# Hymba trunk on one core: quad blocks that accumulate in a kept PSUM bank

## The chip, the core and the metric

The kernel runs on one core of a Trainium2 chip. A time is the device time of one execution in microseconds (us). The kernel before takes 909.75 us, the median of three runs (909.21 to 910.25). Of the engines, TensorE (PE) multiplies, VectorE (DVE) does elementwise arithmetic, ScalarE (ACT) copies and applies functions, GpSimd (POOL) and SyncE (SP) mostly start transfers. Products of TensorE land in PSUM, which the program uses as eight banks of 128 x 512 float32.

## What is computed

Two layers work on 256 tokens of width 1024. Each layer is a half-step feed-forward network (FFN), a mixer of three kinds of heads, and a second half-step FFN, each between two norms:

```python
def _swiglu(h, wg, wu, wd):
    return (jax.nn.silu(h @ wg) * (h @ wu)) @ wd

for l in range(DEPTH):        # DEPTH = 2, D_MODEL = 1024, D_FF = 2816, 256 tokens
    f = _swiglu(_rmsnorm(h, ff1_norm_pre[l]), ff1_w_gate[l], ff1_w_up[l], ff1_w_down[l])
    h = h + 0.5 * _rmsnorm(f, ff1_norm_post[l])
    m = _hybrid_mixer(_rmsnorm(h, mix_norm_pre[l]), ...)
    h = h + _rmsnorm(m, mix_norm_post[l])
    f = _swiglu(_rmsnorm(h, ff2_norm_pre[l]), ff2_w_gate[l], ff2_w_up[l], ff2_w_down[l])
    h = h + 0.5 * _rmsnorm(f, ff2_norm_post[l])
```

## The kernel before

There are four FFNs: FFN1 and FFN2 around the mixer of layer 0, FFN3 and FFN4 around that of layer 1. The gate and up projections have 2816 columns, worked on as 11 units of 256. Units 0 and 1 go first (`ffn_first`); then come three quad blocks of two units each, which begin at units 2, 5 and 8 (`ffn_quad`), and after each of them a pair, which is one unit: 4, 7 and 10 (`ffn_pair`, and `ffn_last_pair` for unit 10). The down projections of a block (`down`, `mm_rows`, L412) run in the block behind it and accumulate in four banks with the tag "acc". All else uses four banks with the tag "wk", handed out in turn.

A float32 product is made of three TensorE products of split operands: the high half (`hi`) of the weights is written by ScalarE (L114), the low half (`lo`) by VectorE (L115) as weights less `hi`; hi·hi, lo·hi and hi·lo accumulate in one bank. The weights' splits are called by `W.pump`, which loads and splits as far as slots are free; `raw`, `hi` and `lo` have five slots each. `pump_behind(m)` places such a call behind the instruction m.

A quad block multiplies a 2 x 2 block of activations by a 2 x 2 block of weights with seven products instead of eight. Each is one call of `product` (L592, its matmul is L598), with sums of activations on the left (`X11`, `S1` to `S4`, `X12`, `X22`) and sums of weights (`g1`, `T1` to `T4`, `g2`, `u2`) on the right; the sums of weights are made by VectorE (L113). Before, four banks are used, in this order of the text: pa takes X11·g1, and ScalarE copies it to `w2` (L609). pc takes S1·T1, copied to `h1` (L614). pb takes S2·T2, and VectorE adds it to `w2` (L625); the sum is subtracted from pc (L626). pd takes S3·T3, and VectorE adds `w2` to it (L637) and subtracts it from `h1` (L638). Then X12·g2 is accumulated onto pa, X22·T4 onto pd, S4·u2 onto pc; ScalarE applies Silu to pa (L647) and pd (L658), VectorE multiplies (L659, L669). The block of unit 8 is called late: its downs are placed otherwise.

The last pair multiplies with the weights on the moving side (`mm_side`). Unit 10's gate columns, then its up columns, each in two halves j = 0 and 1; a half is eight matmuls 512 wide (L359) and eight 256 wide (L361) into one bank. ScalarE copies one part of the bank out (L364), VectorE adds the other (L365). The last pair's activations then go to the downs of the FFN's end.

Results of a block are turned for the downs by a transfer: `send` has ScalarE part the halves of each number (L515) and starts a transposing DMA, `receive` puts them together (L528) and splits them (ScalarE L250, VectorE L251).

A scheduler sets the order on each engine: it starts from the text, estimates durations and may move an instruction of one engine ahead of another where no dependence and no `issue_after` or `keep_in_program_order` speaks against it. A pool gives out banks in turn, and a matmul that starts a bank anew waits until the last reader of what stood there is done.

Of the kernel before, what the change touches and what calls it, by code (L numbers as in the profile page):

```python
# [10 lines left out]
F32 = mybir.dt.float32  # L11
# [23 lines left out]
TAIL = 4  # L35

# [125 lines left out]
def hybrid_trunk_kernel(ctx: ExitStack, tc: tile.TileContext, a, out: bass.AP):  # L162
# [16 lines left out]
    def bank(tag="wk"):  # L179
        return psum.tile([P, 512], F32, tag=tag, name=f"{tag}{next(ids)}")  # L180
# [171 lines left out]
    def mm_side(u, out, between=None):  # L352

        hi, lo = (w[:, :UNIT].rearrange("p (k n) -> p k n", k=KD) for w in W.get(u))
        for j in range(2):
            s = slice(j * P, (j + 1) * P)
            ps = bank()
            for k in range(KD):
                nc.tensor.matmul(ps, hi[:, k, s], both[:, :, k, :], start=k == 0, stop=k == KD - 1)  # L359
            for k in range(KD):  # L360
                mm_side.end = nc.tensor.matmul(ps[:, S:], lo[:, k, s], xT[0][:, k, :], start=False, stop=k == KD - 1,  # L361
                                               skip_group_check=True)
            o = out[:, j * S : (j + 1) * S]
            nc.scalar.activation(o, ps[:, S:], AF.Copy)  # L364
            mm_side.last = nc.vector.tensor_tensor(o, ps[:, :S], o, op=ALU.add)  # L365
            if between and not j:
                between()
        W.done(u)
        return out
# [28 lines left out]
    def mm_rows(acc, u, t, xs, first, last, between=None, at=6, span=(0, 12), pin=False):  # L398

        hi, lo = (w[:, :UNIT].rearrange("p (j n) -> p j n", j=2) for w in W.get(u))  # L400
        if isinstance(xs, dict):
            s = slice(None)
            xh, xl = (x.rearrange("p (j n) -> p j n", n=P)[:, xs["at"] : xs["at"] + 2] for x in xs[t])
# [80 lines left out]
    def ffn_first(t, p, pin=False, ahead=None, between=None, by_dma=False):  # L484

        ps = [bank(), bank()]
# [24 lines left out]
    def send(x, more=False):  # L511

        n = 2 * x.shape[1]
        halves = buf(U16, n)
        part = send.last = nc.scalar.activation(halves.rearrange("p (a n) -> p a n", a=2),  # L515
                                    x[:, :].bitcast(U16).rearrange("p (n a) -> p a n", a=2), AF.Copy)
        turned = buf(U16, n)
        with tc.issue_after(part.ins):
            t = send.dma = nc.sync.dma_start_transpose(turned.rearrange("p (a n) -> p a n", n=P), halves)
        if W.allowed < 10 and not more:  # L520
            W.allowed, W.behind = 10**6, t.ins
        return turned

    def receive(turned):

        n = turned.shape[1] // 2
        x = buf(n=n)
        nc.scalar.activation(x[:, :].bitcast(U16).rearrange("p (n a) -> p a n", a=2), turned.rearrange("p (a n) -> p a n", a=2),  # L528
                             AF.Copy)
        hT = (buf(F32R, n), buf(F32R, n))  # L530
# [13 lines left out]
    def ffn_pair(i, p, turn, take):  # L544

        ps = [bank(), bank()]
# [55 lines left out]
    def ffn_quad(i, p, left, turn, downs, by_dma, two, take=None):  # L602
# [5 lines left out]
        w2 = buf()  # L608
        nc.scalar.activation(w2, pa, AF.Copy)  # L609
# [13 lines left out]
        pb = bank()  # L623
        product(pb, left["S2"], p["T2", i], True)
        nc.vector.tensor_tensor(w2, pb, w2, op=ALU.add)  # L625
# [7 lines left out]
        if not late:  # L633
            downs[0]()
        pd = bank()
        product(pd, left["S3"], p["T3", i], True)
        nc.vector.tensor_tensor(pd, pd, w2, op=ALU.add)  # L637
# [7 lines left out]
        product(pa, left["X12"], p["g2", i], False)  # L645
        h0 = buf()
        nc.scalar.activation(h0, pa, AF.Silu)  # L647
# [33 lines left out]
    def ffn(l, n, p, gain, turned, left, next_left, before_next, last, later=None):  # L681
# [22 lines left out]
        def both(i, behind=None, order=(0, 1)):  # L704
# [5 lines left out]
            else:  # L710
                down(i, 0, behind)
# [53 lines left out]
        xn0 = None if last else before_next(0)  # L765
        for i in range(NU - TAIL, NU):
            if i == NU - 1 and not last:
                pre_turn(0, xn0, left=next_left)
            down(i, 1)
# [7 lines left out]
        W.pump(SPLIT_BUFS - 1)  # L777
# [32 lines left out]
    def mixer(l, p, turned, next_left, before_next):  # L810
# [4 lines left out]
        def first(t, ahead=None):  # L815
            pq, pkv = bank(), bank()
# [62 lines left out]
        def taps(name, tile0):  # L879
            ps = bank()  # L880
# [87 lines left out]
        ps = bank()  # L968
# [58 lines left out]
        pu = bank()  # L1027
# [56 lines left out]
        def zed(t):  # L1084
            ps = bank()
# [39 lines left out]
        def scan(t):  # L1125
            ps = bank()
# [18 lines left out]
        def gated_turn(t, yn):  # L1145
            ps = bank()
# [223 lines left out]
```

## Time and profile before

| | before |
|---|---|
| median of three runs | 909.75 us |
| the profiled execution's own time | 908.51 us |
| its span, first to last instruction | 906.8 us |
| TensorE's mean granted clock | 0.999 of full speed |
| mean DMA rate | 221 GB/s |

A line of a group in the profile names the line of the code, the engine, the operation, the tiles by name (output <- input, numbers left out), shapes and count, then the busy time in us and the mean of one in ns, then the engine's idle time just ahead of it and what ended most of it. A line of a timeline gives start and duration in us of a stretch of instructions, and in brackets the idle time ahead of it. Matmuls are pipelined: a duration of 0.39 us is the way through, and in a row one starts every 0.227 us (256 columns: 0.12). VectorE's and ScalarE's durations overlap a little with the next one's as well.

### The profile page before, as it was taken

How to read it: one execution, taken by the hardware profiler on the slowest of the kernel's cores; microseconds unless marked ns; L12 is line 12 of the kernel's file. 1: busy time of each engine (PE TensorE's matmuls, PEld its weight loads, DVE VectorE, ACT ScalarE, POOL GpSimd, SP SyncE). 2: the span in 40 equal slices, each digit the busy share in tenths (PEclk: the TensorE clock that was granted, in tenths of full speed). 3: DMA queues.
4: the chain of work that ended last, by engine and by line, in shares of the span. 5: the costliest groups of instructions: out<-in, count | busy, mean ns of one | idle time of the engine just before them, and what ended most of it. 6: DMA issues, size and time to landing. Idle time of an engine off the chain costs nothing.

```text
span 906.8 us, 12010 instructions
## 1 busy us (share of the span) xinstructions
PE 897.8 (99%) x4428; PEld 753.8 (83%) x4428; DVE 792.6 (87%) x1044; ACT 673.9 (74%) x1037; POOL 29.9 (3%) x49
## 2 busy tenths in 40 slices
PE   8999999999999999999999999999999999999997
PEld 5888888889988888888888888888998888888885
DVE  6999978899878998988799989888989699989982
ACT  7776776878858777787868678767796668778762
POOL 0000000000001000000000000000000110000000
PEclk9999999999999999999999999999999999999999
DMA  9679888865345489779665978795825256978731
GB/s 365 190 275 265 355 194 278 258 235 183 104 174 219 115 317 228 280 194 284 228 197 152 329 211 299 191 304 212 295 99 166 90 174 182 337 212 299 201 115 47
DMA packets 69326, 200.70 MB, mean 221 GB/s; under 512 B 44306, under 2 KB 44818, under 8 KB 47252
## 3 DMA queue, kind: packets, MB, share of 16 engines
q1 hardware_dynamic: 67396, 187.23, 61.0%
q0 software_dynamic: 1728, 12.58, 7.5%
q8 instruction: 35, 0.57, 0.3%
q14 instruction: 23, 0.19, 0.1%
q10 hardware_dynamic: 144, 0.13, 0.0%
HBM read 188.65 MB, written 1.05 MB: 209 GB/s over the span
## 4 chain that ended last, share of the span: by engine, by line
PE 93%; DVE 4%; issue 2%; ACT 0%; POOLq 0%; POOL 0%; DVEq 0%
PE acc L412 29%; PE wk L598 24%; PE wk L390 13%; PE wk L555 10%; PE wk L350 6%; PE wk L359 3%; DVE lo L115 2%; PE wk L361 2%; PE wk L377 1%; PE wk L301 1%; PE wk L1130 1%; PE acc L873 0%; PE acc L225 0%; DVE raw L113 0%; PE acc L943 0%
## 5 line engine op out<-in xcount | busy, mean ns | idle before, releaser
L115 DVE TENSOR_TENSOR lo<-raw,hi 128x1024 fp32r<-128x1024 f32 (+2 forms) x452 | 465.0, 1079 | 35.1 <-ACT hi L114 34.3
L114 ACT ACTIVATE hi<-raw 128x1024 fp32r<-128x1024 f32 (+2 forms) x452 | 399.1, 937 | 62.4 <-DVE raw L113 26.3
L412 PE MATMUL acc<-hi,t 128*128 128x512 f32 x832 | 214.7, 390 | 0.0
L412 PEld LDWEIGHTS acc<-hi,t 128*128 128x128 f32 x832 | 155.1, 188 | 31.9 <-DVE t L251 0.2
L412 PE MATMUL acc<-lo,t 128*128 128x512 f32 x416 | 113.5, 390 | 0.0
L598 PE MATMUL wk<-hi,n 128*128 128x512 f32 x384 | 100.5, 390 | 0.0
L390 PE MATMUL wk<-hi,xT 128*128 128x512 f32 x384 | 98.6, 393 | 0.0
L412 PEld LDWEIGHTS acc<-lo,t 128*128 128x128 f32 x416 | 78.0, 188 | 16.3
L598 PEld LDWEIGHTS wk<-hi,n 128*128 128x128 f32 x384 | 71.8, 188 | 14.8
L390 PEld LDWEIGHTS wk<-hi,xT 128*128 128x128 f32 x384 | 71.0, 188 | 15.6 <-ACT xT L250 0.7
L598 PE MATMUL wk<-hi,xT 128*128 128x512 f32 x288 | 77.1, 389 | 0.1
L515 ACT ACTIVATE t<-t 128x1024 uint16<-128x1024 uint16 x39 | 41.2, 1056 | 43.7 <-DVE t L669 23.3
L113 DVE TENSOR_TENSOR raw<-raw,raw 128x1024 f32<-128x1024 f32 x56 | 67.0, 1220 | 0.1
L555 PE MATMUL wk<-hi,xT 128*128 128x512 f32 x256 | 64.5, 389 | 0.0
L598 PEld LDWEIGHTS wk<-hi,xT 128*128 128x128 f32 x288 | 54.0, 188 | 11.6 <-DVE t L638 0.4
L555 PEld LDWEIGHTS wk<-hi,xT 128*128 128x128 f32 x256 | 48.1, 188 | 10.0
L528 ACT ACTIVATE t<-t 128x1024 uint16<-128x1024 uint16 x35 | 47.8, 1367 | 8.7 <-DMA t<-t 8.6
L598 PE MATMUL wk<-lo,n 128*128 128x512 f32 x192 | 52.1, 390 | 0.0
L390 PE MATMUL wk<-lo,xT 128*128 128x512 f32 x192 | 52.0, 391 | 0.0
L390 PEld LDWEIGHTS wk<-lo,xT 128*128 128x128 f32 x192 | 36.0, 188 | 8.3 <-DVE lo L115 0.8
L350 PE MATMUL wk<-xT,hi 128*128 128x256 f32 x320 | 42.5, 284 | 0.0
L598 PEld LDWEIGHTS wk<-lo,n 128*128 128x128 f32 x192 | 36.0, 188 | 7.8 <-DVE lo L115 0.2
(190 smaller groups left out, 994.7 us busy)
## 6 DMA issues: line engine op xcount, KB each, us to landing
raw<-in_ff_q SPq DMA_DIRECT2D x48, 1024.0 KB, 6.6
raw<-in_ff_d SPq DMA_DIRECT2D x44, 1024.0 KB, 5.1
raw<-in_ff_f SPq DMA_DIRECT2D x16, 1024.0 KB, 7.2
raw<-in_ff_p SPq DMA_DIRECT2D x16, 1024.0 KB, 4.8
raw<-in_ff_q POOLq DMA_DIRECT2D x12, 1024.0 KB, 8.2
raw<-in_w_in SPq DMA_DIRECT2D x10, 1024.0 KB, 5.1
raw<-in_w_kvz SPq DMA_DIRECT2D x8, 1024.0 KB, 6.7
raw<-in_w_out SPq DMA_DIRECT2D x8, 1024.0 KB, 5.3
```

The lines of the kernel that those rows point to most:

```text
L113: nc.vector.tensor_tensor(raw[:, s], self.raw[x][:, s], self.raw[y][:, s], op=op)
L114: self.act = nc.scalar.activation(hi[:, s], raw[:, s], AF.Copy)
L115: nc.vector.tensor_tensor(lo[:, s], raw[:, s], hi[:, s].bitcast(F32), op=ALU.subtract)
L350: nc.tensor.matmul(ps, w[:, k, s], y[:, k, :], start=i == 0 and k == 0, stop=i == 2 and k == KD - 1)
L359: nc.tensor.matmul(ps, hi[:, k, s], both[:, :, k, :], start=k == 0, stop=k == KD - 1)
L361: mm_side.end = nc.tensor.matmul(ps[:, S:], lo[:, k, s], xT[0][:, k, :], start=False, stop=k == KD - 1, skip_group_check=True)
L390: m = nc.tensor.matmul(ps, y[:, k, :], w[:, k, :], start=h == 0 and n == 0, stop=h == 1 and n == len(parts) - 1)
L412: m = nc.tensor.matmul(acc[b], x[:, j, s], w[:, j, b * 512 : (b + 1) * 512], start=first and j == 0 and i == 0, stop=last and j == 1 and i ...
L515: part = send.last = nc.scalar.activation(halves.rearrange("p (a n) -> p a n", a=2), x[:, :].bitcast(U16).rearrange("p (n a) -> p a n", a= ...
L528: nc.scalar.activation(x[:, :].bitcast(U16).rearrange("p (n a) -> p a n", a=2), turned.rearrange("p (a n) -> p a n", a=2), AF.Copy)
L555: m = nc.tensor.matmul(ps[t], y[:, c, :], w[:, c, :], start=k == 0 and n == 0, stop=k == 1 and n == len(parts) - 1)
L598: nc.tensor.matmul(ps, x[:, k, :], w[:, k, :], start=first and n == 0, stop=n == len(parts) - 1, skip_group_check=not first)
```

## The change

It has five parts. First, the four banks of "wk" become three and one bank with a tag of its own, "keep". Second, in the quad blocks that aren't late (units 2 and 5), X11·g1 still goes to pa, but ScalarE copies it into the kept bank pe instead of `w2`. S2·T2 accumulates onto pa, ScalarE copies the sum from pa to a new `w2`, S3·T3 accumulates onto pa too, and X12·g2 accumulates onto the kept bank pe. VectorE's two additions aren't needed there. Third, the late block stays as it was, with the kept bank for pb. Fourth, the other users of "wk" take the kept bank for one of their banks: the first one in `ffn_first`, the second in `ffn_pair` and in the mixer's `first`, the second half of each unit in `mm_side`, and each fourth bank elsewhere in the mixer (`mbank`). Fifth, the downs of an FFN's last units for the second half of the tokens are placed behind those for the first half, and the call of `W.pump` at the end is placed behind the first half's norm. The code of `send` and `receive` loses a size that is always the same.

```diff
+BANKS = {"wk": 3, "keep": 1, "acc": 4}
...
     def bank(tag="wk"):
-        return psum.tile([P, 512], F32, tag=tag, name=f"{tag}{next(ids)}")
+        return psum.tile([P, 512], F32, tag=tag, name=f"{tag}{next(ids)}", bufs=BANKS[tag])
+
+    turns = iter(range(10**6))
+
+    def mbank():
+        return bank("keep" if next(turns) % 4 == 3 else "wk")
...
         for j in range(2):                                   # mm_side
             s = slice(j * P, (j + 1) * P)
-            ps = bank()
+            ps = bank("keep" if j else "wk")
...
-        ps = [bank(), bank()]                                # ffn_first
+        ps = [bank("keep"), bank()]
...
-        ps = [bank(), bank()]                                # ffn_pair
+        ps = [bank(), bank("keep")]
...
         product(pa, left["X11"], p["g1", i], True)           # ffn_quad
-        w2 = buf()
-        nc.scalar.activation(w2, pa, AF.Copy)
+        pe = w2 = buf() if late else bank("keep")
+        nc.scalar.activation(pe, pa, AF.Copy)
...
-        pb = bank()
-        product(pb, left["S2"], p["T2", i], True)
-        nc.vector.tensor_tensor(w2, pb, w2, op=ALU.add)
+        if late:
+            pb = bank("keep")
+            product(pb, left["S2"], p["T2", i], True)
+            nc.vector.tensor_tensor(w2, pb, w2, op=ALU.add)
+        else:
+            product(pa, left["S2"], p["T2", i], False)
+            w2 = buf()
+            nc.scalar.activation(w2, pa, AF.Copy)
         m = nc.vector.tensor_tensor(pc, pc, w2, op=ALU.subtract)
...
-        if not late:
+        if late:
+            pd = bank()
+            product(pd, left["S3"], p["T3", i], True)
+            nc.vector.tensor_tensor(pd, pd, w2, op=ALU.add)
+        else:
             downs[0]()
-        pd = bank()
-        product(pd, left["S3"], p["T3", i], True)
-        nc.vector.tensor_tensor(pd, pd, w2, op=ALU.add)
+            pd = pa
+            product(pd, left["S3"], p["T3", i], False)
         m = nc.vector.tensor_tensor(h1, h1, pd, op=ALU.subtract)
...
-        product(pa, left["X12"], p["g2", i], False)
+        pg = pa if late else pe
+        product(pg, left["X12"], p["g2", i], False)
         h0 = buf()
-        nc.scalar.activation(h0, pa, AF.Silu)
+        nc.scalar.activation(h0, pg, AF.Silu)
...
-                down(i, 0, behind)                           # ffn
+                both.last = down(i, 0, behind)
...
+        scaled = norm_factor.last
         for i in range(NU - TAIL, NU):
...
-            down(i, 1)
+            down(i, 1, both.last.ins)
...
-        W.pump(SPLIT_BUFS - 1)
+        pump_behind(scaled, SPLIT_BUFS - 1)
...
-            pq, pkv = bank(), bank()                         # mixer
+            pq, pkv = bank(), bank("keep")
```

Three places show what moves. The first is TensorE at FFN1's last pair: gate's second half and then up's two halves, out <- weights or activations, as they stand before.

```order
445 L359 MATMUL wk126_1393<-xT_108,hi37_1280 128x512 [waits Activation_49]
446 L359 MATMUL wk126_1393<-xT_108,hi37_1280 128x512 x7
447 L361 MATMUL wk126_1393<-xT_108,lo37_1281 128x256 x8
448 L359 MATMUL wk131_1420<-xT_108,hi38_1337 128x512 [waits DVE_49,Activation_49]
...
456 L359 MATMUL wk135_1445<-xT_108,hi38_1337 128x512 x8
457 L361 MATMUL wk135_1445<-xT_108,lo38_1338 128x256 x8
```

The same place after the change, where the lines are six further on (L365 and L367 are L359 and L361):

```order
420 L365 MATMUL keep124_1389<-xT_108,hi37_1276 128x512 x8
421 L367 MATMUL keep124_1389<-xT_108,lo37_1277 128x256 x8
422 L365 MATMUL wk129_1416<-xT_108,hi38_1333 128x512 [waits DVE_49,Activation_49]
...
430 L365 MATMUL keep133_1441<-xT_108,hi38_1333 128x512 [waits DVE_49]
431 L365 MATMUL keep133_1441<-xT_108,hi38_1333 128x512 x7
432 L367 MATMUL keep133_1441<-xT_108,lo38_1334 128x256 x8
```

Up's second half had a bank of its own and no wait; it now takes the bank of gate's second half, and its first matmul waits for VectorE, whose add (now L371) reads that bank.

The second is VectorE in FFN1's first quad, from the lo half of a block's result on; `raw4` is a sum of weights, `lo` the weights' low halves. Before:

```order
43 L329 TENSOR_TENSOR t28_216<-t28_216,t27_214 128x512
44 L625 TENSOR_TENSOR t48_416<-wk61_479,t48_416 128x512 [waits PE_49]
45 L251 TENSOR_TENSOR t54_430<-t52_427,t53_429 128x512 [waits Activation_49]
46 L251 TENSOR_TENSOR n58_449<-t35_281,n57_448 128x512 [waits Activation_49]
47 L626 TENSOR_TENSOR wk55_433<-wk55_433,t48_416 128x512 [waits DVE_49,Activation_49]
...
55 L113 TENSOR_TENSOR raw4_291<-raw4_291,raw8_299 128x1024 x2
56 L637 TENSOR_TENSOR wk66_542<-wk66_542,t48_416 128x512 [waits PE_49]
```

After (L335, L257, L635, L114 and L116 are L329, L251, L626, L113 and L115):

```order
43 L335 TENSOR_TENSOR t28_216<-t28_216,t27_214 128x512
44 L114 TENSOR_TENSOR raw4_291<-raw4_291,raw8_299 128x1024 [waits DMAHW4_49,DVE_49]
45 L257 TENSOR_TENSOR t54_430<-t52_427,t53_429 128x512 [waits Activation_49]
46 L257 TENSOR_TENSOR n58_449<-t35_281,n57_448 128x512 [waits Activation_49]
47 L116 TENSOR_TENSOR lo8_458<-raw5_293,hi8_457 128x1024 [waits DMASW0_49,Activation_49]
...
53 L635 TENSOR_TENSOR wk55_433<-wk55_433,t61_491 128x512 [waits Activation_49]
```

The two additions are gone, one half of the weights' sum has moved up to where the first of them stood, and the subtraction from pc has moved down.

The third is TensorE behind FFN2's first pair (L555, now L559); `t387` is the first received tile before, `t384` after. Before:

```order
933 L555 MATMUL wk384_3252<-hi70_3162,xT_108 128x512 x4
934 L598 MATMUL wk399_3411<-hi73_3245,xT_108 128x512 [waits Activation_49]
935 L598 MATMUL wk399_3411<-hi73_3245,xT_108 128x512
936 L598 MATMUL wk399_3411<-hi73_3245,xT_108 128x512 [waits Activation_49]
937 L598 MATMUL wk399_3411<-hi73_3245,xT_108 128x512
938 L598 MATMUL wk399_3411<-lo73_3246,xT_108 128x512 [waits DVE_49]
939 L412 MATMUL acc375_3103<-hi71_3194,t387_3280 128x512 [waits Activation_49]
```

After (L418 is L412):

```order
902 L559 MATMUL keep381_3246<-hi70_3156,xT_108 128x512 x4
903 L418 MATMUL acc373_3099<-hi71_3188,t384_3274 128x512 [waits Activation_49]
904 L418 MATMUL acc374_3100<-hi71_3188,t384_3274 128x512
...
914 L418 MATMUL acc374_3100<-hi71_3188,t385_3275 128x512
915 L418 MATMUL acc373_3099<-hi72_3212,t384_3274 128x512
916 L418 MATMUL acc371_3085<-hi71_3188,t387_3292 128x512 [waits Activation_49]
```

Five matmuls of the next quad's X11 stood between the pair and the downs; now the downs follow the pair at once, and the second received tile (`t387` after) is wanted 13 matmuls later.

More of the change, by code (lines that the diff above doesn't have):

```diff
@@ L402, in mm_rows @@
             s = slice(None)
-            xh, xl = (x.rearrange("p (j n) -> p j n", n=P)[:, xs["at"] : xs["at"] + 2] for x in xs[t])
+            xh, xl = (x.rearrange("p (j n) -> p j n", j=4)[:, xs["at"] : xs["at"] + 2] for x in xs[t])
         else:
@@ L511, in send @@
     def send(x, more=False):
-        n = 2 * x.shape[1]
-        halves = buf(U16, n)
+        halves = buf(U16, 1024)
         part = send.last = nc.scalar.activation(halves.rearrange("p (a n) -> p a n", a=2),
                                     x[:, :].bitcast(U16).rearrange("p (n a) -> p a n", a=2), AF.Copy)
-        turned = buf(U16, n)
+        turned = buf(U16, 1024)
         with tc.issue_after(part.ins):
-            t = send.dma = nc.sync.dma_start_transpose(turned.rearrange("p (a n) -> p a n", n=P), halves)
+            t = nc.sync.dma_start_transpose(turned.rearrange("p (a n) -> p a n", a=8), halves)
         if W.allowed < 10 and not more:
@@ L524, in receive @@
     def receive(turned):
-        n = turned.shape[1] // 2
-        x = buf(n=n)
+        x = buf()
         nc.scalar.activation(x[:, :].bitcast(U16).rearrange("p (n a) -> p a n", a=2), turned.rearrange("p (a n) -> p a n", a=2),
                              AF.Copy)
-        hT = (buf(F32R, n), buf(F32R, n))
+        hT = (buf(F32R), buf(F32R))
         split_into(hT, (slice(None), slice(None)), x)
@@ L879, in taps @@
         def taps(name, tile0):
-            ps = bank()
+            ps = mbank()
             acc = buf()
@@ L965, in mixer @@
         p1 = softmax(s1, 2 * P)
-        ps = bank()
+        ps = mbank()
         nc.tensor.matmul(ps[:, :HEADS], after, dA[:, 0, :], start=True, stop=True)
@@ L1024, in mixer @@
         W.pump()
-        pu = bank()
+        pu = mbank()
         for j in range(2):
@@ L1084, in zed @@
         def zed(t):
-            ps = bank()
+            ps = mbank()
             zed.last = mm_half(ps, [p["z", k] for k in range(2)], t)
@@ L1125, in scan @@
         def scan(t):
-            ps = bank()
+            ps = mbank()
             for hd in range(HEADS):
@@ L1145, in gated_turn @@
         def gated_turn(t, yn):
-            ps = bank()
+            ps = mbank()
             for k in range(4):
```

## The prediction

> **What bounds the kernel now.** I read the page's first line and its part on the chain, then TensorE's waits, then the timelines where the change lets one engine wait for another.
>
> ```profile
> PE 897.8 (99%) x4428; PEld 753.8 (83%) x4428; DVE 792.6 (87%) x1044; ACT 673.9 (74%) x1037; POOL 29.9 (3%) x49
> PE 93%; DVE 4%; issue 2%; ACT 0%; POOLq 0%; POOL 0%; DVEq 0%
> ```
>
> TensorE (PE) is busy for 99% of the span. The chain still gives DVE 4%, some 36 us, which looks like something to win. Whether it is, the waits of PE and of its weight loads tell (line, what was waited for, us in total, times, longest):
>
> ```profile
> PE acc L225 <- DVE zeros L214: 2.3, 1, 2.3
> PE wk L301 <- DVE n L291: 0.2, 1, 0.2
> ...
> PEld wk L598 <- DVE t L638: 0.4, 1, 0.4
> ```
>
> 2.3 us is the first thing that PE does, and the change doesn't touch it. The only other wait of a quad block is 0.4 us behind L638, at 61.03. A chain followed back through such a wait stays on DVE for as long as DVE was busy before it, but removing all of that work gains PE only the wait. So an edit that unloads DVE can gain about 0.5 us here, while each new wait of PE moves the end by its full length, since PE has no idle time left later in which to catch up. The question is therefore: where does the change make PE wait?
>
> **The change: work removed.** These are the groups of all 12 quad blocks (busy us, mean ns):
>
> ```profile
> L637 DVE TENSOR_TENSOR wk<-wk,t 128x512 f32<-128x512 f32 x12 | 8.3, 694 | 0.0
> L625 DVE TENSOR_TENSOR t<-wk,t 128x512 f32<-128x512 f32 x12 | 8.2, 685 | 0.2 <-PE wk L598 0.2
> L609 ACT ACTIVATE t<-wk 128x512 f32<-128x512 f32 x12 | 7.0, 582 | 5.7 <-PE wk L598 5.7
> ```
>
> Eight of the twelve blocks lose L625 and L637: 16 x 0.69 = 11.0 us of DVE. They gain eight ACT copies like L609: 8 x 0.58 = 4.7 us. PE runs the same 4428 matmuls. DVE's 11.0 us lie beside PE and gain at most the wait at 61.03. ACT's 4.7 us are covered by its 26% of idle time. If a copy came late, X12·g2, T3 or T4 would wait for it by at most its length, 0.58. I take 0 for the copies, 0 to 0.58 as bounds. A copy into a kept bank, PSUM to PSUM, isn't in this trace. L609 bounds it from PSUM to SBUF; I take that row.
>
> **The change: one kept bank in the last pair.** This is the large term. mm_side runs gate, then up, each in two halves of eight wide and eight narrow matmuls: four groups. Before, four banks of "wk" take them. Now the second half of gate and the second half of up share the one kept bank. The first matmul of up's second half has to wait until DVE's add (L365) has read gate's second half. When is that matmul due, and when does the add end? FFN1's row of PE first, with the other three behind it, then DVE's adds of gate in all four, then DVE's and ACT's queues in FFN1 (start us, us):
>
> ```profile
> 163.67 2.00 PE L359 MATMUL wk<-xT,hi 128*128 128x512 f32 x8
> ...
> 434.08 1.09 PE L359 MATMUL wk<-xT,hi 128*128 128x512 f32 x4
> ...
> 608.07 1.78 PE L359 MATMUL wk<-xT,hi 128*128 128x512 f32 x7
> ...
> 878.43 1.32 PE L359 MATMUL wk<-xT,hi 128*128 128x512 f32 x5
> ...
> 164.81 0.75 DVE L365 TENSOR_TENSOR t<-wk,t 128x256 f32<-128x256 f32 x2
> ...
> 434.02 0.75 DVE L365 TENSOR_TENSOR t<-wk,t 128x256 f32<-128x256 f32 x2
> ...
> 609.08 0.75 DVE L365 TENSOR_TENSOR t<-wk,t 128x256 f32<-128x256 f32 x2
> ...
> 878.10 0.75 DVE L365 TENSOR_TENSOR t<-wk,t 128x256 f32<-128x256 f32 x2
> ...
> 158.00 6.90 DVE L115 TENSOR_TENSOR lo<-raw,hi 128x1024 fp32r<-128x1024 f32 x6 [2.07 <-ACT hi L114]
> ...
> 155.96 1.06 ACT L515 ACTIVATE t<-t 128x1024 uint16<-128x1024 uint16 x1 [0.76 <-DVE t L659]
> 156.92 5.78 ACT L114 ACTIVATE hi<-raw 128x1024 fp32r<-128x1024 f32 x6
> 162.61 0.63 ACT L364 ACTIVATE t<-wk 128x256 f32<-128x256 f32 x2
> ```
>
> The adds come in twos; the second is that of gate's second half. It ends at 165.56, and the matmul is due at 163.67: 1.89 late. Likewise 434.77 against 434.08 (0.69), 609.83 against 608.07 (1.76), 878.85 against 878.43 (0.42). Sum 4.76 us.
>
> Do the adds come earlier, now that DVE is lighter? The two adds stand behind six lo splits (L115), which follow six hi splits of ACT (L114), and DVE sat idle 2.07 us before them: it waits for ACT. ACT in turn began its six after the send (L515), and sat idle 0.76 us before that, waiting for the gating product of the block, which follows PE's last product. So this stretch hangs on PE, not on DVE's load, and the order on both engines stays the same here. Nothing of the 11 us reaches it.
>
> A wait costs a little more than the lateness. At 61.03 the trace has one:
>
> ```profile
> 60.29 0.68 DVE L638 TENSOR_TENSOR t<-t,wk 128x512 f32<-128x512 f32 x1
> ...
> 59.99 0.93 PE L598 MATMUL wk<-lo,n 128*128 128x512 f32 x3
> 61.03 1.20 PE L598 MATMUL wk<-hi,xT 128*128 128x512 f32 x4
> ...
> 50.93 1.07 PE L598 MATMUL wk<-hi,xT 128*128 128x512 f32 x4
> ```
>
> L638 ends at 60.97 and PE starts 0.06 later; its four matmuls then take 1.20 where four in a row take 1.07, 0.13 more. Together about 0.18. So the term is 4.76 + 4 x 0.18 = **5.5 us**. Behind the waiting matmul stand the rest of up and all downs of the FFN's end, on the one engine that is full. Bounds: 4.8 (no such extra) to 5.9 (0.28 each, were it half as much again).
>
> A rule of the Trainium skill bears on the length of these gaps. Profile first: the clock in the start's gap, as busy time of five engines, clock, DMA share and GB/s.
>
> ```profile
> 4.00:8.00 4.00, 4.00 (x8) 1.66 (x7) 0.75 (x1) 3.48 (x11) 0.56 (x1) 1.00 0.96 365
> ```
>
> Here PE issues only eight matmuls in 4 us, and the granted clock stays at 1.00. The Trainium skill, page "TensorE: Matmul & The Clock Gate", section "What's actually happening", says that TensorE's clock falls to half after one idle window of about 3.4 us. By it none of these waits would lower the clock, and the sum stays; if a shorter gap did it already, a slow window of 3.4 us would cost some 1.7 us, as an estimate from that page, after each. The trace agrees as far as it goes. The rival stands below.
>
> **The change: the first pair's downs.** In FFN 2, 3 and 4 the scheduler had put five matmuls of the next quad's X11 between the first pair and the downs. Now they stand behind. FFN2, PE and then ACT:
>
> ```profile
> 346.85 1.07 PE L598 MATMUL wk<-hi,xT 128*128 128x512 f32 x4
> 347.75 0.39 PE L598 MATMUL wk<-lo,xT 128*128 128x512 f32 x1
> 347.98 1.07 PE L412 MATMUL acc<-hi,t 128*128 128x512 f32 x4
> ...
> 343.79 1.06 ACT L114 ACTIVATE hi<-raw 128x1024 fp32r<-128x1024 f32 x1 [2.41 <-DVE raw L113]
> ...
> 346.93 0.61 ACT L250 ACTIVATE t<-t 128x512 fp32r<-128x512 f32 x1
> 347.46 1.06 ACT L114 ACTIVATE hi<-raw 128x1024 fp32r<-128x1024 f32 x1
> 348.43 1.36 ACT L528 ACTIVATE t<-t 128x1024 uint16<-128x1024 uint16 x1
> 349.82 0.63 ACT L250 ACTIVATE t<-t 128x512 fp32r<-128x512 f32 x1
> ```
>
> The downs need the received tiles: the first half from the L250 at 346.93, the second from the one at 349.82, which ends at 350.45. Now they would start at 346.85 instead of 347.98, and the second tile is due 13 matmuls later, at 346.85 + 13 x 0.227 = 349.80. ACT's stretch was released by DVE (2.41 us of waiting), and DVE is two adds, 1.2 us, earlier, so the first tile comes in time. The hi split between the two (347.46) also waits for the pair's last matmul to free its slot, at about 347.0: from there 0.97 + 1.39 + 0.63 gives 350.0, and 0.18 of release makes it 0.4 late. If DVE's lead doesn't reach ACT, it is 350.45 + 0.18 - 349.80 = 0.8; if the slot is free earlier, 0. I take 0.4, as the slot is the nearest bound: 3 x 0.4 = **1.2 us**, bounds 0 to 2.5.
>
> **The change: FFN1's first quad.** Here DVE is back to back:
>
> ```profile
> 43.06 0.69 DVE L625 TENSOR_TENSOR t<-wk,t 128x512 f32<-128x512 f32 x1
> 43.67 0.69 DVE L251 TENSOR_TENSOR t<-t,t 128x512 fp32r<-128x512 f32 x1
> ...
> 52.88 2.35 DVE L113 TENSOR_TENSOR raw<-raw,raw 128x1024 f32<-128x1024 f32 x2
> ...
> 44.58 1.98 PE L412 MATMUL acc<-hi,t 128*128 128x512 f32 x8
> ```
>
> Where L625 stood (0.60 to the next start), the new order puts a sum of weights (L113, 1.13 each). The lo half behind it (L251) ends 0.53 later, at 44.88, and PE's downs need it at 44.58: 0.30 + 0.18 = 0.48 late. X12·g2 now comes ahead of T3, and the second half of its weights' lo split ends at 50.6, some 0.3 late by the same reckoning. Against these the wait at 61.03 goes (0.47 with its extra): without L625 and L637 ahead of it, L638 ends 1.2 earlier, about 59.8, and PE wanted it near 60.7; nothing else is late there by the rows. Net **+0.3 us**, bounds -0.5 to +0.8.
>
> Elsewhere the kept bank is emptied in time. In the mixer's first products the reader of the kept bank ends at 198.36 and PE wants it at 198.70; I count the other joints at 0.
>
> ```profile
> 197.96 0.40 ACT L826 ACTIVATE t<-wk 128x256 f32<-128x256 f32 x1
> ...
> 198.70 1.09 PE L390 MATMUL wk<-hi,xT 128*128 128x512 f32 x4
> ```
>
> **Sum.** 5.5 + 1.2 + 0.3 = +7.0 us, from the profiled run's 908.5 (span 906.8) to 915.5. The median of three is 909.75, 1.2 above that run, and the same addition gives 916.7.
>
> **Rivals.**
> - The waits in the last pair are there, but the downs and the first quad cost nothing: 5.5 - 0.5, so 914.7. For it: DVE is 1.2 us ahead after each quad, and the two small terms are differences of a few tenths between estimated ends. Against it: FFN1's DVE has no idle time to hide the longer sum.
> - The receives come as late as before and PE waits 0.8 at each pair, and mixers and joints with 0.3 to 0.4 us to spare give a few tenths each: 5.9 + 2.5 + 0.8 + 1 gives +10.2, 919.9.
> - Faster or the same: the kept bank is emptied before it is wanted. That is decided at one place: gate's second add would have to end by 163.5 instead of 165.56 in FFN1, which takes both adds ahead of two of the six lo splits. The lighter DVE would do it only if it were late there; its 2.07 us idle speaks against that. Then only the wait at 61.03 is left, -0.5: 909.3.
> - That the change does nothing to PE (the adds lay beside it, the banks come free in time): 909.75.
> - The gaps lower the clock: if the 16 matmuls behind each of the two long waits (2.00 + 0.95 us apart) ran at half of it, 2 x 2.8 = 5.6 more: 922.3. The clock at 1.00 in the start's gap speaks against it.
>
> **How the numbers follow.** A difference of 0.2%, 1.8 us, is about what a measurement of this kernel can tell from no change. My forecast, 915.5 to 918, has 0.55; only the last pair 0.2; the later receives 0.13; clock 0.02; faster or the same 0.05 each. The range goes from 913.8 (the rival of the last pair alone, with 0.9 for the spread of its waits and of the median) to 919.5. Faster by over 0.2% has 0.03, within 0.2% 0.07, slower 0.9. Predicted: 916.7.
>
> **What would show it.** In the new profile: TensorE's waits list the second half's matmul in mm_side (now L365) behind DVE's add (L371) four times, 5.5 us in all, near 1.9 to 2.1 in FFN1 and FFN3 and 0.6 to 0.9 in FFN2 and FFN4; the downs behind receives three times, 0.4 each; the wait at 61 gone; DVE's busy time down by 11, ACT's up by 5, PE's share of the span about 1% lower. If the four waits aren't there, the forecast falls. If they are there and the end doesn't move, then PE had time to give that its list of waits didn't show.

## The result, and the profile after

| | before | after |
|---|---|---|
| median | 909.66 us (908.66 to 910.25, six runs) | 918.2 us (913.78 to 919.51, six runs) |
| ratio after / before | | 1.0073, 95% interval 1.0055 to 1.0091 |
| the profiled execution's own time | 908.51 us | 913.78 us |
| its span | 906.8 us | 912.1 us |

The change makes the kernel slower. Measured twice more, on two chips, the ratio was 1.0058 (1.0038 to 1.0077) and 1.0040 (1.0026 to 1.0054). The profiled execution was the shortest of the first six, so it shows 5.3 of some 8.5 us; the rest needs an execution of its own, below.

The page of the changed kernel, its first part and the engines' shares of the chain:

```profile
PE 900.8 (99%) x4428; PEld 754.0 (83%) x4428; DVE 782.2 (86%) x1028; ACT 680.5 (75%) x1045; POOL 28.9 (3%) x49
PE 80%; DVE 10%; ACT 4%; issue 4%; DMA 1%; POOL 0%; DVEq 0%; POOLq 0%; SPq 0%; ACTq 0%
```

VectorE lost 10.4 us and ScalarE gained 6.6. TensorE's share of the chain fell from 93 to 80%, as the chain now goes back through its new waits. They stand in the list of TensorE's waits and that of its weight loads (us in total, times, longest us):

```profile
PE keep L365 <- DVE t L371: 1.7, 4, 0.8
...
PEld keep L365 <- DVE t L371: 2.5, 4, 1.0
...
PEld acc L418 <- ACT t L256: 1.7, 3, 0.6
```

Four waits for the kept bank and three for a received tile are there, and the wait at 61 is gone. The four on TensorE's timeline (start, duration, in brackets the idle time):

```profile
165.84 2.11 PE L365 MATMUL keep<-xT,hi 128*128 128x512 f32 x8 [0.80 <-DVE t L371]
...
437.21 2.11 PE L365 MATMUL keep<-xT,hi 128*128 128x512 f32 x8 [0.31 <-DVE t L371]
...
612.22 2.11 PE L365 MATMUL keep<-xT,hi 128*128 128x512 f32 x8 [0.31 <-DVE t L371]
...
883.72 2.11 PE L365 MATMUL keep<-xT,hi 128*128 128x512 f32 x8 [0.31 <-DVE t L371]
```

The bracket counts from the end of the last matmul's way through, so it is less than what is lost: in FFN1 the matmul was due at 164.89 and started at 165.84, 0.95 late, and its eight take 2.11 where the row before the change says 2.00.

What each stage lost is best read from the starts of the same matmul in both traces, which hold 4428 each. This table is worked out from them, in us more than in the profile of before (each column is one profiled execution; what the kernels are is told in the experiments):

| stage, by its times in before | after | a1 | e2 | e1 | e12 | e3 | e5 | before again |
|---|---|---|---|---|---|---|---|---|
| start, 0 to 30 | 0.98 | 0.92 | 0.32 | 1.51 | 1.28 | 0.57 | -0.12 | 0.83 |
| FFN1's first quad, 30 to 66 | 0.29 | 0.27 | 0.28 | 0.29 | 0.29 | 0.01 | 0.28 | -0.01 |
| FFN1's late block and last pair, 145 to 186 | 0.98 | 4.72 | 4.56 | 1.15 | 1.03 | 3.90 | 0.87 | 1.25 |
| first pairs of FFN2 to FFN4 | 1.33 | 1.27 | 0.04 | 1.27 | -0.06 | -0.03 | 1.27 | -0.02 |
| last pairs of FFN2 to FFN4 | 1.71 | 1.69 | 1.71 | -0.03 | -0.03 | 2.63 | -0.03 | -0.03 |
| all else | 0.11 | 0.11 | 0.11 | 0.09 | 0.11 | 0.14 | 2.19 | 0.00 |

### The profile page after: what moved, and what is told of

Read it like the earlier page. It is cut to its first block, busy times and chain, and to the rows that moved or that the text cites. A ratio compares the mean times of both kernels' runs of the same rounds, so it can differ in the third digit from the quotient of the medians.

```text
span 912.1 us, 12006 instructions
## 1 busy us (share of the span) xinstructions
PE 900.8 (99%) x4428; PEld 754.0 (83%) x4428; DVE 782.2 (86%) x1028; ACT 680.5 (75%) x1045; POOL 28.9 (3%) x49
## 4 chain that ended last, share of the span: by engine, by line
PE 80%; DVE 10%; ACT 4%; issue 4%; DMA 1%; POOL 0%; DVEq 0%; POOLq 0%; SPq 0%; ACTq 0%
PE acc L418 26%; PE wk L602 15%; PE keep L396 8%; DVE lo L116 7%; PE wk L396 5%; PE wk L356 5%; PE wk L559 4%; PE keep L559 4%; PE keep L602 3%; ACT hi L115 2%; PE keep L356 1%; PE wk L383 1%; PE wk L307 1%; PE keep L365 1%; DMA raw<-in_ff_q 1%
## 5 line engine op out<-in xcount | busy, mean ns | idle before, releaser
L116 DVE TENSOR_TENSOR lo<-raw,hi 128x1024 fp32r<-128x1024 f32 (+2 forms) x452 | 465.2, 1076 | 49.7 <-ACT hi L115 49.0
L115 ACT ACTIVATE hi<-raw 128x1024 fp32r<-128x1024 f32 (+2 forms) x452 | 400.7, 937 | 70.6 <-DVE raw L114 24.5
L418 PE MATMUL acc<-hi,t 128*128 128x512 f32 x832 | 216.4, 391 | 0.6 <-DVE t L257 0.2
L418 PEld LDWEIGHTS acc<-hi,t 128*128 128x128 f32 x832 | 155.0, 188 | 33.8 <-ACT t L256 1.7
L418 PE MATMUL acc<-lo,t 128*128 128x512 f32 x416 | 113.5, 390 | 0.0
L602 PE MATMUL wk<-hi,n 128*128 128x512 f32 x352 | 93.4, 391 | 0.0
L418 PEld LDWEIGHTS acc<-lo,t 128*128 128x128 f32 x416 | 78.0, 188 | 16.3
L602 PEld LDWEIGHTS wk<-hi,n 128*128 128x128 f32 x352 | 65.8, 188 | 13.5
L114 DVE TENSOR_TENSOR raw<-raw,raw 128x1024 f32<-128x1024 f32 x56 | 67.2, 1217 | 0.1
L602 PE MATMUL wk<-hi,xT 128*128 128x512 f32 x224 | 59.9, 389 | 0.0
L396 PE MATMUL keep<-hi,xT 128*128 128x512 f32 x224 | 59.2, 395 | 0.1
L396 PEld LDWEIGHTS keep<-hi,xT 128*128 128x128 f32 x224 | 41.3, 188 | 10.4 <-ACT hi L115 1.5
L602 PEld LDWEIGHTS wk<-hi,xT 128*128 128x128 f32 x224 | 42.1, 188 | 8.7
L602 PE MATMUL wk<-lo,n 128*128 128x512 f32 x176 | 47.1, 390 | 0.0
L396 PE MATMUL wk<-hi,xT 128*128 128x512 f32 x160 | 41.4, 392 | 0.0
L602 PEld LDWEIGHTS wk<-lo,n 128*128 128x128 f32 x176 | 33.0, 188 | 6.9
L281 DVE TENSOR_TENSOR n<-acc,gains 128x512 f32<-128x512 f32 x24 | 16.1, 686 | 23.1 <-ACT n L264 23.1
L396 PEld LDWEIGHTS wk<-hi,xT 128*128 128x128 f32 x160 | 29.7, 188 | 5.9
L559 PE MATMUL wk<-hi,xT 128*128 128x512 f32 x128 | 34.3, 390 | 0.0
L559 PE MATMUL keep<-hi,xT 128*128 128x512 f32 x128 | 34.2, 389 | 0.0
```

What stands on the lines that cost most here:

```text
L114: nc.vector.tensor_tensor(raw[:, s], self.raw[x][:, s], self.raw[y][:, s], op=op)
L115: self.act = nc.scalar.activation(hi[:, s], raw[:, s], AF.Copy)
L116: nc.vector.tensor_tensor(lo[:, s], raw[:, s], hi[:, s].bitcast(F32), op=ALU.subtract)
L281: nc.vector.tensor_tensor(fg[i], f[i], gains[:, 1, i * 512 : (i + 1) * 512], op=ALU.mult)
L396: m = nc.tensor.matmul(ps, y[:, k, :], w[:, k, :], start=h == 0 and n == 0, stop=h == 1 and n == len(parts) - 1)
L418: m = nc.tensor.matmul(acc[b], x[:, j, s], w[:, j, b * 512 : (b + 1) * 512], start=first and j == 0 and i == 0, stop=last and j == 1 and i ...
```

## The experiments

**The changed kernel again, for its clock.** No edit.

> The changed kernel once more, for its clock. Its profiled run had a span of 912.1 us at a granted clock of 0.998, its other runs 913.7 to 917.8 at 0.999 to 0.994. Theory A (waits of TensorE alone): the span follows the waits, 912 to 913, and a longer one has a lower clock that the waits have nothing to do with. Theory B (waits and clock): the short waits in the last pairs let the granted clock fall in some executions, so that runs lie between 913 and 920 with the clock between 0.994 and 0.999, and the trace shows the lower clock behind one of the waits.

Measured: 915.43 us, six runs in two groups: 913.28, 913.59 and 913.87 at a clock of 0.998 to 0.999, and 917.00, 917.15 and 917.37 at 0.996 to 0.997. The profile is of the second kind. TensorE in FFN1's last pair, and the window behind the wait (busy us and instructions of PE, PEld, DVE, ACT, POOL, then the granted clock, DMA share, GB/s):

```profile
167.97 3.09 PE L365 MATMUL keep<-xT,hi 128*128 128x512 f32 x8 [2.90 <-DVE t L371]
170.87 1.72 PE L367 MATMUL keep<-xT,lo 128*128 128x256 f32 x8
...
169.00:170.00 1.00, 1.00 (x3) 0.72 (x3) 1.00 (x3) 1.00 (x4) 0.00 (x0) 0.50 0.99 377
```

The wait is 3 us long, and behind it the clock is at half, from 168.80 to 172.22 by the trace's record of it: the eight wide matmuls take 3.09 and not 2.0, the eight narrow ones 1.72 and not 1.1. The stage loses 4.72 us in place of 0.98, which is the distance between the two groups of runs. Theory B held, in FFN1 alone. Why is the wait longer? ScalarE's waits for a transfer from 110 us on, in the profile of after and in this one, and VectorE's first split behind it with the end of its work, gate's add of the kept bank:

```profile
ACT hi L115 <- DMA raw<-in_ff_q: 3.0, 1, 3.0
...
132.37 3.50 DVE L116 TENSOR_TENSOR lo<-raw,hi 128x1024 fp32r<-128x1024 f32 x3 [2.84 <-ACT hi L115]
...
165.37 0.42 DVE L371 TENSOR_TENSOR t<-keep,t 128x256 f32<-128x256 f32 x1
```

```profile
ACT hi L115 <- DMA raw<-in_ff_q: 5.2, 1, 5.2
...
134.51 3.50 DVE L116 TENSOR_TENSOR lo<-raw,hi 128x1024 fp32r<-128x1024 f32 x3 [5.08 <-ACT hi L115]
...
167.51 0.41 DVE L371 TENSOR_TENSOR t<-keep,t 128x256 f32<-128x256 f32 x1
```

From the first split to the end of the add it is 33.42 us in the one and 33.41 in the other. So in FFN1 VectorE sets the add's end from the moment at which GpSimd's accumulating transfer lands, and TensorE, whose matmul is due at 164.9 in both, waits for what is left over. GpSimd issues the transfer at 123.0 us in both; what differs is the time that it takes. Between 110 and 136 us, first after and then this profile (KB, us from issue to landing):

```profile
raw<-in_ff_q POOLq DMA_DIRECT2D x1, 1024.0 KB, 8.2
...
raw<-in_ff_q POOLq DMA_DIRECT2D x1, 1024.0 KB, 10.4
```

**Up's second half in a bank of its own.**

```diff
-            ps = bank("keep" if j else "wk")
+            ps = bank("keep" if j and not between else "wk")     # between: up only
```

> The changed kernel, but the second half of up in the last pairs takes a bank of wk and not the kept one, so that it doesn't wait for VectorE's add of gate's second half. Both theories: the four waits of 1.07 and 3 x 0.58 us go, 2.8 us less at the same clock. Theory A: median 2.8 lower than the changed kernel, near 915.4, with the same spread. Theory B: the clock stays at 0.998 or above in all runs, median near 911 to 912.

Measured: 911.24 us, ratio 1.0015 (1.0005 to 1.0026), the clock at 0.998 to 1.000 in eleven of twelve runs. The four waits are gone. Its transfer was as late as a1's (ScalarE waited 5.2 us), yet FFN1's stage lost 1.15 and not 4.72, as before itself did in its second profile (below): that is what VectorE's lateness costs through the received tile of the downs when no bank holds TensorE back first. This bank alone makes 4.2 of the 5.5 us by which a1's median lies above before, as theory B said. (That median lies between a1's two groups; against the middle run of each the edit gains 2.4 and 5.9 us.)

**The downs of both units for one half of the tokens first.** Behind FFN2's to FFN4's first pair:

```diff
-                for b in before:
+                if i == PAIRS[0] and order == (1, 0):
+                    for b in before:
+                        end = down(b, order[0], u)
+                    with tc.issue_after(end.ins):
+                        hT[i] = receive(sent.pop())
+                    for b in before:
+                        down(b, order[1], u)
...
+                else:
+                  for b in before:
                     both(b, u, order)
```

> The changed kernel, but behind the first pair of FFN2 to FFN4 the downs of both units run for the one half of the tokens before those for the other half, so that the second received tile is wanted 24 matmuls after the pair and not 13. Both theories: the three waits of 0.41 us go, 1.2 us less at the same clock. Theory A: median near 917.0. Theory B, if the waits in the last pairs are what lowers the clock: near 917, clock as low as the changed kernel's; if the waits behind the first pairs do it too: less.

Measured: 913.48 us, ratio 1.0034 (1.0018 to 1.0049), clock 0.997 to 0.999. The first pairs' loss goes from 1.27 to 0.04 us, 1.2 less as expected; the last pairs' stays, and so does FFN1's 4.56 with the low clock. That the median is nearly 2 us below a1's and not 1.2 lies within the two groups' mixture.

**Both edits.**

> Both edits together. The waits that are left are those of FFN1's first quad, 0.4 us more than before, and up to 0.9 us at the start that one profile showed. Theory A: 2.8 + 1.2 = 4.0 below the changed kernel, near 914.2. Theory B: the clock stays at 0.998 or above, and the median is within 1 us of before, 909.7 to 910.7.

Measured: 909.91 us, ratio 0.9996 (0.9985 to 1.0006). With the two waits gone the changed kernel is level with the one before. No version was faster than before.

**The kernel before, again.**

> The kernel before once more, as a kernel of its own, for a second profile. The accumulating transfer into raw (GpSimd's queue) in FFN1's second pair released ScalarE at 130.7 in the profile of before; in the five profiles of changed kernels ScalarE waited 3.0 us for it once and about 5 us four times. Theory A (the transfer's time varies from execution to execution, whatever the kernel): this profile may show 3 or 5, and TensorE doesn't wait in FFN1's last pair either way, since its four banks are distinct, or less than 1 us. Theory B (the change delays the transfer): 3.0 as before. Also the start: the first 30 us took 30.0 in before and 0.3 to 1.5 more in the five; if that is the transfers' chance, this profile lies anywhere from 30 to 31.5.

Measured: 908.99 us, ratio 1.0002 (0.9993 to 1.0011). Its profile lost 0.83 us at the start and 1.25 in FFN1's last pair against the first profile, with no edit at all. ScalarE waited 2.9 us for the transfer, as in the first profile, but it was late itself: VectorE's split behind the transfer starts at 133.83 and not at 131.79, 2.04 us later, where TensorE was 0.81 later. From that split to the end of gate's second add it is 33.8 us in both. So the 1.25 us come down the same chain, through the received tile of the downs:

```profile
168.02 0.97 PE L412 MATMUL acc<-hi,t 128*128 128x512 f32 x3 [0.49 <-ACT t L250]
```

So the start's 0.98 us in after needn't be the change's (e5, with the same start, lost none there), and VectorE's chain in FFN1 can come late in either kernel. The late landing itself (5 us of waiting) was seen in changed kernels alone, in four of the nine that had no work added ahead of the transfer: there it took 10.3 to 10.5 us from GpSimd's issue to ScalarE's start, and 8.1 to 9.5 in the other five and in both profiles of before. The four are those of one chip, and no profile of before is known to be from that chip. Whether the change makes the late landing likelier stays open.

**The banks alone, with VectorE's additions back.**

```diff
-        pe = w2 = buf() if late else bank("keep")
+        pe = w2 = buf()
...
-        if late:
-            pb = bank("keep")
...
+        pb = bank("keep")
+        product(pb, left["S2"], p["T2", i], True)
+        nc.vector.tensor_tensor(w2, pb, w2, op=ALU.add)
...
+        pd = bank()
+        product(pd, left["S3"], p["T3", i], True)
+        nc.vector.tensor_tensor(pd, pd, w2, op=ALU.add)
```

> The changed kernel's banks, order of the downs and joints, but all quad blocks add on VectorE as before (pb in the kept bank), so that VectorE has its 11 us back. Theory A (the forecast's: gate's add in the last pairs hangs on TensorE, not on VectorE's load): the waits of the last pairs are those of the changed kernel, 1.07 or 3.3 in FFN1 and 0.58 in each of FFN2 to FFN4. Theory B (VectorE's load in the late block sets it): they are 0.8 in FFN2, 1.9 in FFN3 and 0.6 in FFN4, about 1.6 us more in all, and at 1.9 us the clock may fall behind it.

Measured: 915.39 us, ratio 1.0076 (1.0051 to 1.0101). The banks cost at least as much without the new arithmetic as with it. The last pairs of FFN2 to FFN4 lose 2.63 us in place of 1.71, and FFN1's wait is over 2 us though its transfer was early (2.5 us of waiting):

```profile
166.57 3.06 PE L365 MATMUL keep<-xT,hi 128*128 128x512 f32 x8 [2.22 <-DVE t L371]
...
614.20 2.11 PE L365 MATMUL keep<-xT,hi 128*128 128x512 f32 x8 [0.75 <-DVE t L371]
```

VectorE's load does count: with it the waits are longer, by 0.9 us in the three. But FFN3 has 0.99 and not the 1.9 that theory B had from the first trace; there the first trace's lateness was particular to that execution (gate's second add ended 1.76 us after the matmul's start in it, 0.63 in the second profile of before). Neither theory had the sizes. Behind the 2.2 us the clock fell here too.

**TensorE's gap filled.** Twelve matmuls of zeros between the halves of up in FFN1; they compute nothing.

```diff
+            if j and between and not mm_side.filled:
+                mm_side.filled = True
+                idle = bank()
+                for _ in range(12):
+                    m = nc.tensor.matmul(idle, zeros[:, :P], zeros, start=True, stop=True)
+                    tc.keep_in_program_order(m)
             ps = bank("keep" if j else "wk")
```

> The changed kernel with twelve matmuls of zeros between the halves of up in FFN1's last pair alone, 12 x 0.227 = 2.7 us of TensorE's time, work that is of no use. If the 3 us without matmuls make the clock fall to half for the 2.9 us behind it, this costs nothing where the transfer is late: the stretch is longer than before by 3.2 us and not by 4.7, with the clock at 1.00 behind it, 1.5 us less than the changed kernel. If the clock fell for another reason, the stretch is longer by 4.7 as it was. Where the transfer is early, 1.7 us are lost: 2.7 in place of 1.0.

Measured: 914.76 us, runs of 914.37 to 915.56, the clock at 0.998 to 0.999 in all. The profile had an early transfer, so it doesn't show the case for which the fill was meant. What it shows in the runs is the missing second group: with the gap filled none lies above 915.6, where the changed kernel had runs of 917 to 919.5. That fits the low clock as the gap's doing, but four runs on one chip don't show it: the changed kernel itself, measured a third time (below), had none above 913.9. The profile lost 2.6 us in FFN1's last pair, near the 2.7 expected, and 1.6 in FFN3's in place of 0.6: there GpSimd's transfer took 10.3 us from issue to landing, 8.2 in after, and TensorE's matmul came 1.5 us late. So a late transfer lengthens the wait in another FFN too.

**The downs no longer held back.** The fifth part of the change undone, as to the downs:

```diff
-                both.last = down(i, 0, behind)
+                down(i, 0, behind)
...
-            down(i, 1, both.last.ins)
+            down(i, 1)
```

> The changed kernel, but the downs for the second half of the tokens are no longer held behind those for the first half. The scheduler then puts 12, 8, 9 and 3 of their matmuls between the halves of up in FFN1 to FFN4: 2.7, 1.8, 2.0 and 0.7 us of useful work in the place of the wait. Theory A (the kept bank's wait is lost whatever stands behind): nothing changes. Theory B (the wait costs only since the fifth part of the change holds back the work that could fill it): the three waits of 0.58 go, FFN1's falls to 0.4 at most, no low clock behind it; median near 912, as with up in a bank of wk.

Measured: 913.32 us, ratio 1.0045 (1.0032 to 1.0058), five runs of 912.86 to 913.59, clock 0.998 to 0.999. The scheduler puts useful matmuls into the gap, and all four waits for the kept bank are gone. So the wait is lost time only since the fifth part takes away the work that could stand there. But the median didn't reach 912: some 3 us come back elsewhere, 2.19 in the table's last row and the 0.87 of FFN1's row, which is a wait at 183.6 us, in the joint behind FFN1, and not one of the last pair. Most of it is in the joints, where the same matmuls had covered the norms; L307 is TensorE's first product on a norm's output, and in after it waits 0.2 us once.

```profile
PE wk L307 <- DVE n L297: 1.3, 2, 0.7
```

**The changed kernel a third time.**

> The changed kernel a third time. By the theory that the runs so far leave: an execution whose accumulating transfer in FFN1's second pair is early has a wait of about 1 us in FFN1's last pair, a clock of 0.998 or 0.999 and 912.5 to 914.5 us; one whose transfer is late has a wait of more than 2 us there, the clock at half for some 3 us behind it, 0.996 or 0.997, and 916.5 to 918 us; and the runs above 918 at 0.994 or 0.995 have a second wait of more than 2 us with a low clock behind it, in another last pair. A profile of such a run would show it. The rival: they are runs of one long low clock for another cause, or with a later start.

Measured: 913.29 us, all five runs at 912.24 to 913.89 and 0.998 to 0.999. The transfer was waited for by 3.6 us, TensorE's gap in FFN1 was 1.5, and the clock stayed at 1.00 behind it. All runs are of the first group, so nothing was learned of those above 918.

**The transfer delayed, in both kernels.** GpSimd adds zeros to the tile ahead of FFN1's second pair's accumulating transfer, in the changed kernel and in the one before:

```diff
+            self.thens = getattr(self, "thens", 0) + 1
+            if self.thens == 3:
+                for c in range(0, UNIT, 256):
+                    x = self.raw[then[0]][:, c : c + 256]
+                    nc.gpsimd.tensor_tensor(x, x, self.nought, op=ALU.add)
             nc.gpsimd.dma_start(self.raw[then[0]][:, :UNIT], then[1], accum_op=ALU.add)
```

> The changed kernel, but GpSimd adds zeros to the raw tile, eight times 128x256, ahead of the accumulating transfer of FFN1's second pair alone, so that it starts some 2 to 5 us later (the additions' time isn't known); the order on TensorE and VectorE stays. Theory A (VectorE is back to back from the splits behind that transfer to gate's adds, 34.5 us in three profiles of the changed kernel, so each us of lateness is a us of TensorE's wait): ScalarE waits 5 to 8 us for the transfer in place of 3.0 to 5.2, the wait in FFN1's last pair is as much longer, 3 to 6 us, the clock is at half for some 3 us behind it in every execution, and the runs lie together at 917 to 921 us with a clock of 0.997 or below. Theory B (the late transfer and the long wait only occur together): the wait stays at 1.0 to 1.4 or 3.0, and the runs at 912 to 918.

> The same additions ahead of the same transfer in the kernel before. Its gate and up halves have four banks, so TensorE waits for no add of gate; what is late is the received tile of the downs behind the last pair, which was 0.9 us late in the second profile of before. Theory A: the same 2 to 5 us of delay cost the kernel before that much less the room that it has there, so 0 to 4 us, and the difference between the two kernels under this delay is 3 us and more of the wait and 1.5 of the clock, unless TensorE waits over 2 us for the received tile too. Theory B: no change, 909 to 910.

Measured: 923.93 us (922.71 to 924.08) and 918.5 (918.24 to 918.98). The additions took far longer than I had allowed for, and ScalarE waited 9.5 us:

```profile
120.30 11.30 POOL L124 TENSOR_TENSOR raw<-raw,nought 128x256 f32<-128x256 f32 x8 [43.31 <-DVE raw L114]
...
141.04 3.50 DVE L116 TENSOR_TENSOR lo<-raw,hi 128x1024 fp32r<-128x1024 f32 x3 [8.35 <-ACT hi L115]
...
174.01 0.41 DVE L378 TENSOR_TENSOR t<-keep,t 128x256 f32<-128x256 f32 x1
...
174.48 3.69 PE L372 MATMUL keep<-xT,hi 128*128 128x512 f32 x8 [2.94 <-DVE t L378]
```

From split to add it is 33.38 us again: the transfer does set the add. But the wait in the last pair didn't grow past 3.1 us, since with so late a transfer TensorE already waits in the late block, in both kernels (they lose 4.2 and 4.4 us between 66 and 145), and comes later itself. Two of these waits, from the changed kernel's list and from before's (L609 and L605 are `product`'s matmul):

```profile
PE keep L609 <- ACT hi L115: 1.8, 1, 1.8
...
PE wk L605 <- DVE wk L633: 2.3, 1, 2.3
```

The clock fell behind the first waits of the late block, in both kernels. Between 145 and 186 the changed kernel loses 7.57 us and before 4.62. The direction of theory A holds, its range of times (917 to 921) doesn't.

## Why the prediction was right, and where its sizes were not

The sign, the range and the mechanism came out: 918.2 us lies in 913.8 to 919.5, near the predicted 916.7, and the four waits in the last pairs plus the three behind the first pairs are the loss, since a kernel with both taken away is level with before. That the number came so near is partly luck: the last pairs come near the sum's 5.5 us only in executions with a late transfer and a low clock, and the sum had neither. The changed kernel's other two medians lie 5.5 and 4.3 us above those of before measured beside them, where 7.0 were forecast, and the lower one, 913.29, lies outside the range. Term by term:

- **Work removed and copies: 0.** Right. The 10 us that VectorE lost gained nothing on TensorE beyond the wait at 61.
- **The last pairs: 5.5 us. The mis-sized term.** In the profile it measures 0.96 + 3 x 0.47 in front of the waiting matmul and 4 x 0.11 behind it, 2.8 us. In an execution like a1's it is 1.7 in FFN2 to FFN4 and, with the clock, some 3.6 in FFN1 (4.72 less e1's 1.15): 5.3. The step that failed is "this stretch hangs on PE, not on DVE's load": I followed ScalarE's second send one step back and stopped. One step further stood, in the timeline of before, ScalarE and then VectorE:

```profile
153.66 1.06 ACT L515 ACTIVATE t<-t 128x1024 uint16<-128x1024 uint16 x1 [5.17 <-DVE t L669]
154.62 0.58 ACT L658 ACTIVATE t<-wk 128x512 f32<-128x512 f32 x1
...
148.40 4.62 DVE L115 TENSOR_TENSOR lo<-raw,hi 128x1024 fp32r<-128x1024 f32 x4
152.94 0.69 DVE L669 TENSOR_TENSOR t<-wk,t 128x512 f32<-128x512 f32 x1
```

  The Silu (L658) that the chain needs stands behind a send that waited 5.17 us for VectorE, and VectorE was back to back. In FFN1 the chain hangs on VectorE and the transfer; TensorE was 1.2 us later there in after (start and first quad) and ScalarE's send only 0.2, so part of the earlier loss was given back in a shorter wait. In after the lighter VectorE waited for TensorE in the late block of FFN2, FFN3 and FFN4, as it had in before's FFN4 alone (the last line):

```profile
414.99 0.69 DVE L630 TENSOR_TENSOR t<-keep,t 128x512 f32<-128x512 f32 x1 [1.10 <-PE keep L602]
...
590.00 0.69 DVE L630 TENSOR_TENSOR t<-keep,t 128x512 f32<-128x512 f32 x1 [0.95 <-PE keep L602]
...
861.49 0.69 DVE L630 TENSOR_TENSOR t<-keep,t 128x512 f32<-128x512 f32 x1 [0.18 <-PE keep L602]
...
856.68 0.69 DVE L625 TENSOR_TENSOR t<-wk,t 128x512 f32<-128x512 f32 x1 [0.21 <-PE wk L598]
```

  From there to the end of gate's second add it is 22.2 us in all four. So the wait falls to 0.47 us, the same in FFN2, FFN3 and FFN4 and near what FFN4 had shown before (0.42 late): the floor that TensorE sets itself. e3, with VectorE's load back, has 0.67, 0.91 and 0.75. Nor were the latenesses of the first trace the kernel's own: 1.89, 0.69, 1.76 and 0.42 in FFN1 to FFN4 are 3.03, 1.02, 0.63 and 0.42 in the second profile of before. Only FFN4's, which hangs on TensorE, stays.
- **The first pairs: 1.2 us.** Right, 1.33 by the table, and for the reason given: ScalarE sits idle until TensorE frees the slot, and the tile comes 0.4 late.

```profile
349.25 1.07 ACT L115 ACTIVATE hi<-raw 128x1024 fp32r<-128x1024 f32 x1 [0.68 <-PE keep L559]
```

- **FFN1's first quad: 0.3 us.** Right, 0.27 to 0.29 in six profiles with the new arithmetic and 0.01 without it, and in after its three parts measure 0.45, 0.28 and -0.47, near the 0.48, 0.3 and -0.47 of the forecast.
- **The rival of the clock, with a chance of 0.02.** Underrated. In about half of a1's runs, and in the profiles of a1, e2 and e3, it came true in FFN1, some 1.6 us each time (1.09 on the eight wide matmuls and 0.6 on the narrow ones in a1, less the 0.1 of a restart). I had set against it the clock of 1.00 between 4 and 8 us in before. That row is no evidence: matmuls there start 0.42 us apart (six from 2.32, the next line at 4.86), twice the 0.227 of the rest, so TensorE did run at half speed where the row says 1.00. The trace's record of the clock begins only at 7.37 us.

```profile
2.32 2.74 PE L225 MATMUL acc<-zeros 128*128 128x512 bf16 x6 [2.32 <-DVE zeros L214]
```

- **The rivals of faster or no change.** They fell: gate's second add ended at 165.79, not by 163.5.

What stays open: the first six runs had two above 919 at a clock of 0.994 and 0.995, some 2 us beyond what one late transfer and one low clock explain; no profile fell on such a run. A second late transfer with a second low clock could make up the 2 us, and e4's FFN3 shows that transfers can come late elsewhere; that those runs had one isn't shown.

## What to carry to other kernels

Where one engine has no idle time, count banks and not only instructions: an edit that takes 10 us from an engine with time to spare gains nothing, and one bank fewer at a place where four had been in flight costs a wait that can't be caught up. Follow each chain back until an engine is reached that really sat idle, since an operation behind the right product may still queue behind a wait for another engine. And when an order is held fixed, ask which wait the scheduler was filling with that work: here the same matmuls covered either the last pairs or the joints.

## What the runs showed of the hardware

Short gaps lowered TensorE's clock. By the distances of the matmuls in all thirteen profiles (0.427 us apart and not 0.227), no gap of up to 1.5 us after the start was followed by half speed, while those of 2.4 (e3), 3.0 (e2) and 3.1 us (a1, e7) in the last pair were, 0.05 (e7) to 0.9 us after the restart, and for some 3.4 us. In the late block of e7 and e8, gaps of 1.9 and 2.4 us were followed by it, 1.8 and 1.0 us after the restart, and gaps of 1.8 and 2.4 us, 12 us behind those, were not: length alone doesn't decide.

The records of the granted clock in these traces show what does. In each of the thirteen, the clock's changes lie whole multiples of 3.413 us apart, so an execution falls into windows of that length; the first change comes at 4.96 to 8.34 us, so the windows lie elsewhere in each. The six windows ahead of a fall to half within the kernel had 1.87 to 2.94 us without a matmul in flight, by the durations in the trace (a1: 2.59 in the window from 165.39 to 168.80). The falls at the kernel's end follow windows with 2.59 us or more. Of the 3400 windows without a fall behind them none had more than 1.84 (e4, near its end). The gap of 2.4 us that cost nothing in e8 lies across two windows, with 1.31 and 0.97 us in them. So in these runs a gap cost the clock when it took more than about half of one window: its place counts as well as its length.

The Trainium skill, page "TensorE: Matmul & The Clock Gate", section "What's actually happening", gives one idle window of about 3.4 us as what halves the clock, and a busy one of that length as what restores it. The traces agree with the half and with the length of the slow stretch. They differ on what starts it: here a window with 1.87 us without matmuls was enough once.

GpSimd took 1.41 us for each addition of 128x256 float32 (11.30 for eight), more than three times the 0.42 us that VectorE took for an add of that shape with one operand in PSUM (L371).
